# Cross-attention of the samples: values summed on VectorE in PSUM, two heads at a time

## The chip, the cores and the metric

The kernel runs on one core of a Trainium2 chip. The metric is the device time of one execution in microseconds; lower is better. All times below are microseconds unless marked otherwise. TensorE is also called PE, VectorE DVE, ScalarE ACT, GpSimd POOL; SP is the queue that issues most DMAs.

## The reference

One step of a two-layer decoder trunk, f32 throughout, for two groups that share all weights: a prompt of 256 rows and 8 samples of one row each. Each layer is four residual blocks: SwiGLU, a mixer (a gated short convolution in layer 0, a gated linear recurrence in layer 1), cross-attention to a memory of 256 rows, SwiGLU again. What matters here is the cross-attention of the samples, whose keys and values come from a cache, each sample with its own:

```python
def cross_attn(x, mk, mv, w_q, w_o):          # samples: B=8, T=1; mk, mv: (8, 256, 4, 256)
    B, T, D = x.shape
    q = (x @ w_q).reshape(B, T, X_HEADS, X_HEAD_DIM)            # 4 heads of 256
    s = jnp.einsum('bthd,bnhd->bhtn', q, mk) / math.sqrt(X_HEAD_DIM)
    p = jax.nn.softmax(s, axis=-1)
    o = jnp.einsum('bhtn,bnhd->bthd', p, mv).reshape(B, T, D)
    return o @ w_o
```

The prompt does the same against keys and values that are projected from `mem_prompt` in the kernel; those are outputs too.

## The kernel before, in words

Activations stand transposed, `xT[:, k]` holding 128 of the 1024 features over 264 columns: 256 prompt rows, then the 8 samples. Every f32 matrix is split into a high and a low part (`wh`, `wl` of a weight; `xh`, `xl` of an activation), and a product is three matmuls (`mm3`, L326 to L330). Weights arrive in halves of four 128-row blocks: SP loads a half into `raw` (L96), ScalarE rounds it to `wh` (L107), and VectorE or POOL makes `wl` (L120). Which of the two does that is `W.lo`: `("v",)` or `("p",)`.

The order of issue is set by `Flow`. Three lanes hold generators; `flow.tick()` first advances the weights by one split, one round and the loads that fit, and then takes one step of the first generator of each lane. The projections call `tick` once every few matmuls, so other work is spread between them.

The `Ring` has four slots of 1 MB in SBUF (128 x 2048 f32). Its line is fixed: for each layer eight slots of cached keys, eight of cached values, then four of recurrent states. When a slot is given back (`ring.done`) the next load of the line is issued on SP at once. All loads of SP, of weights and of the ring, stand in one queue.

One `attention(l, ...)` runs so:

- `project(XH, ...)` makes the four heads' queries (`qT`). At each head's end `sample_scores(h)` goes to lane 0, and after the last head `sample_rest()`.
- `do_kv(h)`, four times, projects the prompt's keys and values (L930 to L932, tile `kv`) with `W.lo = ("p",)`. Each head ticks eight times, and at its end puts three generators on lane 1: `transpose_k` (tiles `pkt`, `KTt`), `prompt_scores` (`psc`, `mxp`, `Pp`, `ppt`, `PTh`, `PTl`) and `prompt_values` (`po`, then the prompt columns of `oh` and `ol`).
- `sample_scores(h)`: a partition holds 16 of the 256 cached rows of one sample (16 partitions a sample, 8 samples). For each of its 16 rows `i`, VectorE multiplies the key by the query and adds up along the row (L984), giving `sc[:, h, i]`.
- `sample_rest()`: the softmax over `sc` (maxima and sums across a sample's 16 partitions go through small matmuls, tile `pst`). Then `Ps` (L1072) is each weight, divided by the sum and laid out with 8 columns, zero but for the partition's own sample (`own`). TensorE multiplies `Ps[:, h, i]` with the values of row `i` and head `h`, 64 f32 products a layer in four groups (L1086, tile `spv`; a f32 product shows as two records), all into one PSUM bank, head `h` on partitions from 32`h`. ScalarE copies the sums to `os` (L1097), TensorE transposes that (L1101, tile `spt`), and the result goes to the sample columns of `oh` and `ol` (L1104, L1105).
- After the last head `flow.drain(0)` issues what is left of lane 0, `W.lo` goes back to `("v",)`, and `out_proj` (through `project_late`, with `k0` = 6) multiplies `oh` and `ol` by the output weights: the first two chunks over k = 0 to 5, the third over the same, then, once lane 1 is drained (`ready`), k = 6 and 7 of them and the fourth chunk. Columns k = 2h and 2h + 1 belong to head h.

PSUM has eight banks here: four for projections (`mm_bank`) and four for everything else (`aux_bank`); two of the latter hold the third chunk in `project_late`. The framework's scheduler makes the final order on each engine from the order of issue and what is ready, and sets all waits.

Of the kernel before, what the change touches and what calls it, by code (L numbers as in the profile page):

```python
# [8 lines left out]
F32 = mybir.dt.float32  # L9
# [3 lines left out]
ALU = mybir.AluOpType  # L13
# [3 lines left out]
P = 128  # L17
D = 1024
KT = D // P
T = 256  # L20
NB = 8
# [4 lines left out]
XH = 4  # L26
XD = 256
RH = 8
NI = NMEM * NB // P
# [6 lines left out]
HK = 4  # L36
# [203 lines left out]
def trunk_step(ctx: ExitStack, tc: tile.TileContext, ins, consts, outs, stop=None):  # L240
    nc = tc.nc
# [7 lines left out]
    def mm_bank(name):  # L249
        return pmm.tile([P, 512], F32, tag="mm", name=name)  # L250

    def aux_bank(name):
        return paux.tile([P, 512], F32, tag="aux", name=name)

    W = Weights(nc, wp)
    flow = Flow(W)
    ring = Ring(cp)

    ident = cp.tile([P, P], F32, name="ident")
# [4 lines left out]
    own = cp.tile([P, NB], F32, name="own")  # L264
# [67 lines left out]
    class Norm:  # L332
# [55 lines left out]
        def ready(self):  # L388
            if not self.done:
                flow.drain(2)  # L390
# [57 lines left out]
                    evac(c, j, ps[:, :NC])  # L448
                flow.tick()

    def project_late(nch, rh, rl, evac, k0, ready):

        lead = 3
        first = W.chunks[W.pos]
        ws = [W.get_late() for _ in range(lead)]
        pss = [[(mm_bank if c < 2 else aux_bank)(f"pj{c}_{j}") for j in range(2)] for c in range(lead)]

        def block(c, k):
            for j in range(2):
                mm3(pss[c][j][:, :NC], ws[c](k), rh[:, k], rl[:, k], k == 0, k == KT - 1, slice(j * P, j * P + P))  # L460

        for k in range(k0):
            for c in range(2):
                block(c, k)
            if k == HK - 1:
                W.first_live = first[0] + 2
            flow.tick()
        for k in range(k0):
            block(2, k)
            if k == HK - 1:  # L470
                W.first_live = first[1]
            if k % 2:
                flow.tick()
        ready()

        def leave(c, j, ps):
            with tc.high_priority(offset=HURRY):
                evac(c, j, ps[:, :NC])

        def finish(c):  # L480
            for k in range(k0, KT):
                block(c, k)
            W.first_live = first[1] + c + 1
            for j in range(2):
                leave(c, j, pss[c][j])
            flow.tick()

        for c in range(lead - 1):
            finish(c)
        w = W.get_late()  # L490
        for j in range(2):
            ps = mm_bank(f"pj{lead}_{j}")
            for k in range(KT):
                mm3(ps[:, :NC], w(k), rh[:, k], rl[:, k], k == 0, k == KT - 1, slice(j * P, j * P + P))
                if k == KT // 2 - 1:
                    flow.tick()
            if j == 1:
                W.release()
            leave(lead, j, ps)
            flow.tick()  # L500
            if j == 0:
                finish(lead - 1)
# [222 lines left out]
    def add_cache(l):  # L725
        def fill_k(h, hf):
            def f(t):
                rows = ins["cache_mem_k"][l].rearrange("b (g i) h d -> (b g) i h d", i=NI)
                nc.sync.dma_start(t.rearrange("p (i d) -> p i d", d=XD), rows[:, 8 * hf : 8 * hf + 8, h])

            return f

        def fill_v(i2):
            def f(t):
                rows = ins["cache_mem_v"][l].rearrange("b (g i) h d -> (b g) i (h d)", i=NI)
                nc.sync.dma_start(t.rearrange("p (i e) -> p i e", i=2), rows[:, 2 * i2 : 2 * i2 + 2])

            return f

        for h in range(XH):  # L740
            for hf in range(2):
                ring.add((l, "k", h, hf), fill_k(h, hf))
        for i2 in range(NI // 2):
            ring.add((l, "v", i2), fill_v(i2))

    def add_states(key):
        def fill(p):
# [63 lines left out]
    def out_proj(rh, rl, nxt, before=None, late=None):  # L811
        def evac(c, j, ps):
            k = 2 * c + j
            add = nc.vector.tensor_add(xT[:, k], xT[:, k], ps)
            if k == KT - 1:
                W.after["v"] = add.ins
                nxt.low(k - 1)
            nxt.kt(k, low=k != KT - 2)

        if late is not None:  # L820
            project_late(4, rh, rl, evac, *late)
        else:
            project(4, rh, rl, evac, before=before)
# [64 lines left out]
    def attention(l, norm, nxt):  # L888
        with tc.tile_pool(name="at", bufs=1) as ap:
# [3 lines left out]
            oh = ap.tile([P, KT, NC], F32R, name="oh")  # L893
            ol = ap.tile([P, KT, NC], F32R, name="ol")
            sc = ap.tile([P, XH, NI], F32, name="sc")
            Ps = ap.tile([P, XH, NI, NB], F32, name="Ps")
            os = ap.tile([P, XD], F32, name="os")
            nc.gpsimd.memset(os, 0.0)
            tops = ap.tile([P, P], F32, name="tops")
            nc.gpsimd.memset(tops, 0.0)  # L900

# [149 lines left out]
            def sample_rest():  # L1051

                mx, zs, rz = (ap.tile([P, XH], F32, name=n) for n in ("mxs", "zss", "rzs"))
                top = ap.tile([XH, NB], F32, name="top")
                nc.vector.reduce_max(mx, sc, axis=AX.X)
                yield
                pt = aux_bank("pst")
                nc.tensor.transpose(pt[:XH, :P], mx, ident)
                nc.vector.reduce_max(top, pt[:XH, :P].rearrange("h (b g) -> h b g", b=NB), axis=AX.X)
                nc.vector.tensor_copy(tops[:XH].rearrange("h (b g) -> h b g", b=NB), spread(top))  # L1060
                yield
                nc.tensor.matmul(pt[:, P : P + XH], tops, ident[:, :XH], start=True, stop=True)
                nc.vector.tensor_scalar(mx, pt[:, P : P + XH], -1.0 / 16.0, None, op0=ALU.mult)
                for h in range(XH):
                    act(
                        sc[:, h], sc[:, h], AF.Exp, bias=mx[:, h : h + 1], scale=1.0 / 16.0, accum_out=zs[:, h : h + 1]
                    )
                yield
                nc.tensor.matmul(pt[:, P + XH : P + 2 * XH], peers, zs, start=True, stop=True)
                nc.vector.reciprocal(rz, pt[:, P + XH : P + 2 * XH])  # L1070
                for h in range(XH):
                    nc.vector.scalar_tensor_tensor(  # L1072
                        Ps[:, h],
                        sc[:, h].unsqueeze(2).broadcast_to([P, NI, NB]),
                        rz[:, h : h + 1],
                        own.unsqueeze(1).broadcast_to([P, NI, NB]),
                        op0=ALU.mult,
                        op1=ALU.mult,
                    )
                yield  # L1080
                ps = aux_bank("spv")
                for i in range(0, NI, 4):
                    for at in (2, 0, 1, 3):
                        t = ring.tiles[l, "v", (i + at) // 2].rearrange("p (i h d) -> p i h d", i=2, h=XH)
                        for h in range(XH):
                            nc.tensor.matmul(  # L1086
                                ps[32 * h : 32 * h + NB, :XD],
                                Ps[:, h, i + at],
                                t[:, at % 2, h],
                                start=i == 0 and at == 2,  # L1090
                                stop=i == NI - 4 and at == 3,
                            )
                    for i2 in (i // 2, i // 2 + 1):
                        ring.done((l, "v", i2))
                    yield
                for h in range(XH):
                    nc.scalar.copy(os[32 * h : 32 * h + NB], ps[32 * h : 32 * h + NB, :XD])  # L1097
                yield
                pt = aux_bank("spt")
                for dt in range(2):  # L1100
                    nc.tensor.transpose(pt[:, dt * P : dt * P + P], os[:, dt * P : dt * P + P], ident)  # L1101
                ptv = pt[:, : 2 * P].rearrange("p (t h r) -> p h t r", t=2, r=32)[:, :, :, :NB]
                ohv, olv = (t[:, :, T:].rearrange("p (h t) b -> p h t b", t=2) for t in (oh, ol))
                nc.scalar.copy(ohv, ptv)  # L1104
                nc.vector.tensor_sub(olv, ptv, ohv.bitcast(F32))  # L1105

            flow.spawn(1, mem_split())
            project(XH, xh, xl, evac_q, need=norm)
            W.lo = ("p",)
            for h in range(XH):  # L1110
                do_kv(h)
            flow.drain(0)
            W.lo = ("v",)
            out_proj(oh, ol, nxt, late=(KT - 2, lambda: flow.drain(1)))


    GH = 4
# [425 lines left out]
    for i, e in enumerate(plan):  # L1543
        if i + 1 < len(plan):
            nxt = Norm(*plan[i + 1][:3])
        else:
            nxt = Final() if stop is None else Stop()
# [60 lines left out]
```

## Time and profile before

| | us |
|---|---|
| median of 3 runs | 1299.87 (1298.6 to 1300.09) |
| the profiled execution, its own time | 1299.62 |
| its span in the profile | 1297.8 |

The profile is one execution. A group's row gives line, engine, operation, output and inputs with their shapes, the count, then busy us and mean ns of one, then the idle time of the engine just before them and what ended it. A row of an engine's work in order of time gives start, duration, engine, line, operation, output and inputs, count and, in brackets, the idle time before it. Rows of the chain that ended last give start, duration and work. Matmuls overlap, so their pace is read from start to start, not from their durations. The granted TensorE clock was 0.996 over the span.

In layer 0 the attention's kv heads run from 328.2 to 392.8 and out_proj from there to 422.6; in layer 1 the groups `spv` run from 1026.3 to 1050.1.

### The profile page before, as it was taken

To read this page: it belongs to the slowest core of one execution; us is meant where nothing else is said; L and a number is where in the kernel's file an instruction comes from. 1 tells how busy PE (TensorE), PEld (TensorE's weight loads), DVE (VectorE), ACT (ScalarE), POOL (GpSimd) and SP (SyncE) were. 2 spreads that over 40 slices of the span, in tenths; PEclk is the share of its full clock that TensorE was granted. 3 is DMA by queue.
4 is the path that set the end of the run, shared out by engine and by line. 5 is a ranking of instruction groups with operands and counts; after the bars stand their busy time and mean duration, and the time that the engine had idled before them with its cause. 6 is when DMAs were issued, how large, how long until landed. Compare 5 with 4: busy or idle time off the path is not lost.

```text
span 1297.8 us, 25932 instructions
## 1 busy us (share of the span) xinstructions
PE 1276.5 (98%) x10306; PEld 1238.1 (95%) x10306; DVE 824.1 (64%) x1564; ACT 694.3 (53%) x1138; POOL 294.8 (23%) x238
## 2 busy tenths in 40 slices
PE   8999999999999999999999999999999999999997
PEld 8999999999869999999999999999998789999996
DVE  6655567759926755556655545888789637666454
ACT  6455545446545645534554544656675447666542
POOL 3211231212650211132111132000023521211220
PEclk9999999999999999999999999999999999999999
DMA  8695555646998666556566556564557995777650
GB/s 284 225 300 179 168 182 181 196 147 195 360 369 252 187 179 180 179 164 201 178 189 179 173 177 187 163 199 127 179 163 256 399 333 144 232 211 203 202 165 34
DMA packets 263099, 266.75 MB, mean 206 GB/s; under 512 B 8697, under 2 KB 259577, under 8 KB 260930
## 3 DMA queue, kind: packets, MB, share of 16 engines
q1 hardware_dynamic: 257150, 259.78, 64.0%
q10 hardware_dynamic: 5828, 5.32, 1.2%
q8 instruction: 81, 1.33, 0.4%
q14 instruction: 40, 0.33, 0.1%
HBM read 255.00 MB, written 10.07 MB: 204 GB/s over the span
## 4 chain that ended last, share of the span: by engine, by line
PE 92%; DVE 4%; ACT 2%; issue 1%; DMA 0%; POOL 0%; DVEq 0%; SPq 0%; ACTq 0%; POOLq 0%
PE pj L328 19%; PE pj L329 19%; PE pj L330 19%; PE dn L328 7%; PE dn L330 7%; PE dn L329 7%; PE kv L931 2%; PE kv L930 2%; PE kv L932 2%; DVE xl L353 2%; DVE wl L120 1%; PE spv L1086 1%; PE psc L1012 1%; PE pl L1250 1%; PE pj L406 1%
## 5 line engine op out<-in xcount | busy, mean ns | idle before, releaser
L120 DVE TENSOR_TENSOR wl<-raw,wh 128x1024 fp32r<-128x1024 f32 (+1 forms) x347 | 426.3, 1233 | 245.9 <-ACT wh L107 231.4
L328 PE MATMUL pj<-xh,wh 128*128 128x264 f32 x1952 | 558.7, 286 | 5.1 <-DVE qT L916 2.5
L329 PE MATMUL pj<-xl,wh 128*128 128x264 f32 x1952 | 553.2, 284 | 0.0
L330 PE MATMUL pj<-xh,wl 128*128 128x264 f32 x1952 | 552.9, 283 | 0.0
L107 ACT CAST wh<-raw 128x1024 fp32r<-128x1024 f32 (+1 forms) x406 | 416.3, 1032 | 253.1 <-PE pj L329 128.4
L328 PEld LDWEIGHTS pj<-xh,wh 128*128 128x128 f32 x1952 | 367.7, 188 | 7.3 <-DVE qT L916 3.0
L329 PEld LDWEIGHTS pj<-xl,wh 128*128 128x128 f32 x1952 | 367.9, 189 | 0.0
L330 PEld LDWEIGHTS pj<-xh,wl 128*128 128x128 f32 x1952 | 366.1, 188 | 0.0
L328 PE MATMUL dn<-ah,wh 128*128 128x264 f32 x704 | 200.9, 285 | 0.0
L330 PE MATMUL dn<-ah,wl 128*128 128x264 f32 x704 | 200.0, 284 | 0.0
L329 PE MATMUL dn<-al,wh 128*128 128x264 f32 x704 | 199.4, 283 | 0.0
L780 POOL TENSOR_TENSOR al<-a,ah 128x264 fp32r<-128x264 f32 x88 | 90.2, 1026 | 418.8 <-ACT ah L779 418.7
L120 POOL TENSOR_TENSOR wl<-raw,wh 128x1024 fp32r<-128x1024 f32 (+1 forms) x61 | 142.8, 2350 | 183.9 <-ACT wh L107 122.3
L330 PEld LDWEIGHTS dn<-ah,wl 128*128 128x128 f32 x704 | 132.7, 188 | 0.0
L328 PEld LDWEIGHTS dn<-ah,wh 128*128 128x128 f32 x704 | 132.4, 188 | 0.2
L329 PEld LDWEIGHTS dn<-al,wh 128*128 128x128 f32 x704 | 132.5, 188 | 0.0
L308 ACT ACTIVATE g<-g 128x264 f32<-128x264 f32 x88 | 37.0, 424 | 80.7 <-DVE g L772 80.5
L779 ACT CAST ah<-a 128x264 fp32r<-128x264 f32 x88 | 36.0, 413 | 65.2 <-DVE a L778 65.0
L348 ACT ACTIVATE xh<-xT,gains 128x264 fp32r<-128x264 f32 x56 | 28.2, 513 | 74.2 <-DVE xT L806 59.2
L984 DVE CUSTOM_DVE_ANT_0 junk<-ring,pq 128x256 f32<-128x256 f32 x128 | 53.7, 419 | 3.7
L778 DVE TENSOR_TENSOR a<-g,pj 128x264 f32<-128x264 f32 x88 | 37.1, 426 | 28.7 <-PE pj L330 28.6
L772 DVE TENSOR_TENSOR g<-pj,R_norm_ffn 128x264 f32<-128x264 f32 x88 | 37.5, 429 | 25.7 <-PE pj L330 25.3
(330 smaller groups left out, 1495.6 us busy)
## 6 DMA issues: line engine op xcount, KB each, us to landing
raw<-in_w_ffn_gate_dram SPq DMA_DIRECT2D x88, 512.0 KB, 4.7
raw<-in_w_ffn_up_dram SPq DMA_DIRECT2D x88, 512.0 KB, 4.0
raw<-in_w_ffn_down_dram SPq DMA_DIRECT2D x64, 512.0 KB, 3.5
ring<-in_cache_mem_k_dram SPq DMA_DIRECT2D x16, 1024.0 KB, 8.2
raw<-in_w_xkv_dram SPq DMA_DIRECT2D x64, 256.0 KB, 3.7
ring<-in_cache_mem_v_dram SPq DMA_DIRECT2D x16, 1024.0 KB
raw<-in_w_rec_in_dram SPq DMA_DIRECT2D x32, 512.0 KB, 4.6
raw<-in_w_ffn_down_dram SPq DMA_DIRECT2D x32, 384.0 KB, 3.0
```

Of the source, the lines that this page charges most:

```text
L107: self.pin(self.behind(self.hi[i % len(self.hi)], copy(wh[:, :n], self.raw[i][:, :n])))
L120: ins = eng.tensor_sub(wl[:, :n], self.raw.pop(i)[:, :n], wh[:, :n].bitcast(F32))
L308: in_line(nc.scalar.activation(dst, src, func, **kw))
L328: nc.tensor.matmul(ps, wh[:, s], rh, start=first, stop=False)
L329: nc.tensor.matmul(ps, wh[:, s], rl, start=False, stop=False)
L330: nc.tensor.matmul(ps, wl[:, s], rh, start=False, stop=last)
L348: W.pin(nc.scalar.activation(xh[:, k, :n], src, AF.Copy, scale=gcol(self.name, self.layer, k)))
L772: nc.vector.tensor_mul(g, ps, norm.R)
L778: nc.vector.tensor_mul(a, g, ps)
L779: nc.scalar.copy(ah[:, blk], a)
L780: nc.gpsimd.tensor_sub(al[:, blk], a, ah[:, blk].bitcast(F32))
L984: nc.vector.tensor_tensor_reduce(junk, t[:, i % 8], pq[:, :XD], 1.0, 0.0, ALU.mult, ALU.add, sc[:, h, i : i + 1])
```

## The change

TensorE no longer multiplies `Ps` with the values. For each pair of heads VectorE keeps two running sums side by side in one PSUM bank (`acc`): row by row `i`, and head by head within it, it multiplies the values with the partition's own weight `sc[:, h, i]` and adds the sum so far. The last row's result goes to SBUF (`total`). That leaves one sum for each partition, 16 for a sample; four f32 products a pair, with `total` as the weights and the 8 columns of `oz` (one over the softmax's sum in the partition's own sample, zero elsewhere), add those up across partitions and transpose at once. The copies to `oh` and `ol` follow for each pair.

A slot of cached values now holds four rows of two heads and not two rows of four heads, so that a pair needs four slots. `flow.drain(0)` is gone: `project_late` asks for pair 0 before k = 0 and for pair 1 before k = 4, through `until`, and does k = 0 to 3 of all three chunks before k = 4 and 5. `W.lo` changes to `("v",)` only at the second of these.

```diff
-    def project_late(nch, rh, rl, evac, k0, ready):
+    def project_late(nch, rh, rl, evac, k0, need, ready):
...
-        for k in range(k0):
-            for c in range(2):
-                block(c, k)
-            if k == HK - 1:
-                W.first_live = first[0] + 2
-            flow.tick()
-        for k in range(k0):
-            block(2, k)
-            if k == HK - 1:
-                W.first_live = first[1]
-            if k % 2:
+        for a, b in ((0, HK), (HK, k0)):
+            need(a)
+            for k in range(a, b):
+                for c in range(2):
+                    block(c, k)
+                if k == HK - 1:
+                    W.first_live = first[0] + 2
                 flow.tick()
+            for k in range(a, b):
+                block(2, k)
+                if k == HK - 1:
+                    W.first_live = first[1]
+                if k % 2:
+                    flow.tick()
         ready()
...
-        def fill_v(i2):
+        def fill_v(pair, i4):
             def f(t):
                 rows = ins["cache_mem_v"][l].rearrange("b (g i) h d -> (b g) i (h d)", i=NI)
-                nc.sync.dma_start(t.rearrange("p (i e) -> p i e", i=2), rows[:, 2 * i2 : 2 * i2 + 2])
+                at = slice(2 * pair * XD, 2 * pair * XD + 2 * XD)
+                nc.sync.dma_start(t.rearrange("p (i e) -> p i e", i=4), rows[:, 4 * i4 : 4 * i4 + 4, at])
...
-                for h in range(XH):
-                    nc.vector.scalar_tensor_tensor(Ps[:, h], ...)
+                nc.vector.tensor_mul(
+                    oz,
+                    rz.unsqueeze(2).broadcast_to([P, XH, NB]),
+                    own.unsqueeze(1).broadcast_to([P, XH, NB]),
+                )
                 yield
-                ps = aux_bank("spv")
-                for i in range(0, NI, 4):
...
-                            nc.tensor.matmul(
-                                ps[32 * h : 32 * h + NB, :XD],
-                                Ps[:, h, i + at],
-                                t[:, at % 2, h],
...
+                for pair in range(XH // 2):
+                    acc = aux_bank("acc")
+                    total = ap.tile([P, 2, XD], F32, tag="total", name="total", bufs=1)
+                    for i in range(NI):
+                        t = ring.tiles[l, "v", pair, i // 4].rearrange("p (i h d) -> p i h d", i=4, h=2)
+                        for j in range(2):
+                            p, sums = sc[:, 2 * pair + j, i : i + 1], acc[:, j * XD : j * XD + XD]
+                            if i == 0:
+                                nc.vector.tensor_scalar(sums, t[:, i % 4, j], p, None, op0=ALU.mult)
+                            else:
+                                dst = total[:, j] if i == NI - 1 else sums
+                                nc.vector.scalar_tensor_tensor(
+                                    dst, t[:, i % 4, j], p, sums, op0=ALU.mult, op1=ALU.add
+                                )
+                        if i % 4 == 3:
+                            ring.done((l, "v", pair, i // 4))
+                        if i % 2:
+                            yield
+                    pt = aux_bank("spt")
+                    for j in range(2):
+                        for dt in range(2):
+                            at = (2 * j + dt) * NB
+                            nc.tensor.matmul(
+                                pt[:, at : at + NB],
+                                total[:, j, dt * P : dt * P + P],
+                                oz[:, 2 * pair + j],
+                                start=True,
+                                stop=True,
+                            )
+                    ptv = pt[:, : 4 * NB].rearrange("p (t b) -> p t b", b=NB)
+                    ohv, olv = (t[:, 4 * pair : 4 * pair + 4, T:] for t in (oh, ol))
+                    nc.scalar.copy(ohv, ptv)
+                    nc.vector.tensor_sub(olv, ptv, ohv.bitcast(F32))
+                    sampled.add(pair)
                     yield
+
+            def until(pair):
+                while pair not in sampled:
+                    flow.step()
+                if pair:
+                    W.lo = ("v",)
...
-            flow.drain(0)
-            W.lo = ("v",)
-            out_proj(oh, ol, nxt, late=(KT - 2, lambda: flow.drain(1)))
+            out_proj(oh, ol, nxt, late=(KT - 2, lambda k: until(k // 4), lambda: flow.drain(1)))
```

More of the change, by code (lines that the diff above doesn't have):

```diff
@@ L742, in add_cache @@
                 ring.add((l, "k", h, hf), fill_k(h, hf))
-        for i2 in range(NI // 2):
-            ring.add((l, "v", i2), fill_v(i2))
+        for pair in range(XH // 2):
+            for i4 in range(NI // 4):
+                ring.add((l, "v", pair, i4), fill_v(pair, i4))
     def add_states(key):
@@ L895, in attention @@
             sc = ap.tile([P, XH, NI], F32, name="sc")
-            Ps = ap.tile([P, XH, NI, NB], F32, name="Ps")
-            os = ap.tile([P, XD], F32, name="os")
-            nc.gpsimd.memset(os, 0.0)
+            oz = ap.tile([P, XH, NB], F32, name="oz")
+            sampled = set()
             tops = ap.tile([P, P], F32, name="tops")
@@ L1070, in sample_rest @@
                 nc.vector.reciprocal(rz, pt[:, P + XH : P + 2 * XH])
-                for h in range(XH):
[L1072 to L1079, printed above, removed]
-                yield
@@ L1081, in sample_rest @@
-                ps = aux_bank("spv")
-                for i in range(0, NI, 4):
[L1083 to L1086, printed above, removed]
-                                ps[32 * h : 32 * h + NB, :XD],
-                                Ps[:, h, i + at],
-                                t[:, at % 2, h],
-                                start=i == 0 and at == 2,
-                                stop=i == NI - 4 and at == 3,
-                            )
-                    for i2 in (i // 2, i // 2 + 1):
-                        ring.done((l, "v", i2))
-                    yield
@@ L1096, in sample_rest @@
[L1096 to L1103, printed above, removed]
@@ L1104, in sample_rest @@
-                nc.scalar.copy(ohv, ptv)
-                nc.vector.tensor_sub(olv, ptv, ohv.bitcast(F32))
+                nc.vector.tensor_mul(
[3 more added lines that the diff above has]
+                )
+                yield
+                for pair in range(XH // 2):
+                    acc = aux_bank("acc")
[19 more added lines that the diff above has]
+                            at = (2 * j + dt) * NB
+                            nc.tensor.matmul(
+                                pt[:, at : at + NB],
[3 more added lines that the diff above has]
+                                stop=True,
+                            )
+                    ptv = pt[:, : 4 * NB].rearrange("p (t b) -> p t b", b=NB)
[3 more added lines that the diff above has]
+                    sampled.add(pair)
+                    yield
```

## The prediction, made before the run

> **What bounds the kernel now.** I read the page's busy shares and the chain first, then the stretches of layer 0's attention, then each engine in order of time there. Layer 1's attention holds the same groups of instructions, so every term counts twice.
>
> ```profile
> PE 1276.5 (98%) x10306; PEld 1238.1 (95%) x10306; DVE 824.1 (64%) x1564; ACT 694.3 (53%) x1138; POOL 294.8 (23%) x238
> PE 92%; DVE 4%; ACT 2%; issue 1%; DMA 0%; POOL 0%; DVEq 0%; SPq 0%; ACTq 0%; POOLq 0%
> ```
>
> TensorE holds 92% of the chain: work taken off it shortens the run, unless another engine becomes late. The samples' products are such work:
>
> ```profile
> L1086 PE MATMUL spv<-ring,Ps 128*8 128x256 f32 x256 | 15.3, 379 | 0.0
> ```
>
> Where they run, VectorE is nearly free (columns: busy us of PE, PEld, DVE, ACT, POOL, then clock, DMA share, GB/s):
>
> ```profile
> 360.00:370.00 10.00, 10.00 (x93) 6.34 (x92) 3.99 (x10) 3.20 (x13) 3.90 (x2) 1.00 1.07 408
> 370.00:380.00 10.00, 10.00 (x64) 7.96 (x67) 2.08 (x3) 6.21 (x10) 5.30 (x3) 1.00 1.01 411
> 380.00:390.00 10.00, 9.97 (x88) 6.55 (x77) 0.18 (x1) 3.77 (x7) 6.62 (x3) 1.00 1.03 274
> 390.00:400.00 10.00, 10.00 (x70) 9.17 (x70) 5.01 (x11) 4.93 (x12) 0.00 (x0) 1.00 1.17 321
> 400.00:410.00 10.00, 10.00 (x79) 9.79 (x78) 5.74 (x10) 4.33 (x9) 0.00 (x0) 1.00 1.01 341
> ```
>
> TensorE has no gap from 360 to 410, and VectorE is busy for 11.3 of the 40 us to 400. The DMA engines are full throughout. So the question is whether that free VectorE time, 28.7 us, holds the new sums before TensorE asks for them.
>
> **The change part by part.** Off TensorE: eight groups of products (four a layer), and the two transposes of `os`.
>
> ```profile
> 359.32 0.38 PE L1062 MATMUL pst<-ident,tops 128*128 128x4 f32 x2 [0.16 <-DVE tops L1060]
> 359.56 0.48 PE L931 MATMUL kv<-wl,mh 128*128 128x512 f32 x1
> ...
> 363.00 0.39 PE L931 MATMUL kv<-wl,mh 128*128 128x512 f32 x1
> 363.23 0.40 PE L932 MATMUL kv<-wh,ml 128*128 128x512 f32 x1
> 363.56 1.91 PE L1086 MATMUL spv<-ring,Ps 128*8 128x256 f32 x32
> 365.40 0.50 PE L930 MATMUL kv<-wh,mh 128*128 128x512 f32 x1
> ...
> 388.68 0.39 PE L930 MATMUL kv<-wh,mh 128*128 128x512 f32 x1
> 389.10 0.44 PE L1101 MATMUL spt<-ident,os 128*128 128x128 f32 x2
> 389.37 0.60 PE L960 MATMUL pkt<-ident,Kn 128*128 128x128 f32 x4
> ...
> 392.82 0.28 PE L328 MATMUL pj<-oh,wh 128*128 128x264 f32 x1
> 422.51 0.28 PE L330 MATMUL pj<-oh,wl 128*128 128x264 f32 x1
> ```
>
> From start to start, 363.23 to 365.40 is 2.17; less one product of kv (0.23, 363.00 to 363.23) a group costs 1.94. The transposes: 389.37 - 388.68 - 0.23 = 0.46. A layer loses 4 x 1.94 + 0.46 = 8.2.
>
> On to TensorE: four products a pair with `total` as the weights and 8 columns, each f32 product being two records (as L1062 is). The nearest row is L1062: two records from 359.32 to 359.56, 0.12 each. 8 x 0.12 = 0.96 a pair, 1.9 a layer. The net is 6.3 a layer, 12.6 in all.
>
> On to VectorE: 64 instructions a layer over 128x256, two heads in turn, each reading its own last sum. No VectorE instruction of before writes PSUM; the nearest rows:
>
> ```profile
> L353 DVE SCALAR_TENSOR_TENSOR xl<-px,gains,xh 128x256 fp32r<-128x256 f32 x8 | 3.3, 472 | 0.2 <-ACT xh L348 0.2
> 310.70 1.27 DVE L908 SCALAR_TENSOR_TENSOR ml<-memT,gains,mh 128x256 fp32r<-128x256 f32 x3
> 312.03 0.43 DVE L319 SCALAR_TENSOR_TENSOR nacc_norm_xattn<-ps_ms,R_norm_xattn 128x264 f32<-128x264 f32 x1
> 312.50 0.43 DVE L323 SCALAR_TENSOR_TENSOR nacc_norm_xattn<-nacc_norm_xattn,R_norm_xattn 128x264 f32<-128x264 f32 x1
> 362.26 1.14 DVE L1072 SCALAR_TENSOR_TENSOR Ps<-sc,rzs,own 128x128 f32<-128x128 f32 x4
> ```
>
> One takes 0.472, from PSUM as from SBUF. Three that need nothing of each other take 1.27, so they follow at (1.27 - 0.47) / 2 = 0.40. One that needs its predecessor follows at 0.47 after a duration of 0.43, that is 0.04 behind its end: 0.51 for this shape. These are the two ends. I take 0.40, the lower: with two heads in turn the sum that an instruction needs was begun 0.80 earlier, and the L1072 rows, all into one tile, overlap too (four in 1.14). 64 x 0.40 = 25.6; the four Ps (1.14) go, one small product (`oz`) comes.
>
> [...]
>
> The rest of VectorE's work between 362.3 and the moment the second pair is wanted:
>
> ```profile
> L964 DVE COPY KTt<-pkt 128x512 f32<-128x512 f32 x8 | 5.5, 687 | 1.5 <-PE pkt L960 1.5
> L996 DVE TENSOR_REDUCE mxp<-psc 128x2 f32<-128x512 f32 x8 | 5.5, 690 | 6.3 <-PE psc L1012 6.3
> L997 DVE TENSOR_SCALAR mxp<-mxp 128x2 f32<-128x2 f32 x8 | 2.2, 272 | 0.2
> L1004 DVE TENSOR_SCALAR Pp<-Pp,zsp 128x256 f32<-128x256 f32 x16 | 7.1, 488 | 0.2
> L1033 DVE TENSOR_TENSOR PTl<-ppt,PTh 128x512 fp32r<-128x512 f32 x8 | 5.5, 690 | 12.9 <-ACT PTh L1032 12.9
> L948 DVE TENSOR_TENSOR Vl<-Vn,Vh 128x512 fp32r<-128x512 f32 x8 | 5.5, 689 | 6.9 <-ACT Vh L947 6.9
> L1049 DVE TENSOR_TENSOR ol<-po,oh 128x512 fp32r<-128x512 f32 x8 | 5.5, 682 | 1.5 <-ACT oh L1048 1.5
> ```
>
> Head 1 from mxp to ol: 0.69 + 0.27 + 0.98 + 0.69 + 0.68 = 3.3. Head 2 the same with KTt: 4.0. Vl of heads 2 and 3: 1.4. Head 3's KTt and mxp: 1.65. `oz`, reciprocals and the small `ol`, an estimate of 1.0 from L997's size. Together 11.3. The sums then end at 362.3 + 25.6 + 11.3 = 399.2, and with the last pair's products (0.96) and the copies to oh and ol (0.5, an estimate from the smallest rows above) the second pair is there at about 400.7.
>
> TensorE asks for it at k = 4 of out_proj:
>
> ```profile
> 397.29 0.44 PE pkt L960 x4
> 400.01 1.73 PE psc L1012 x8
> ...
> 409.35 0.28 PE L328 MATMUL po<-PTh,Vh 128*128 128x256 f32 x1
> 410.77 0.29 PE L328 MATMUL pj<-oh,wh 128*128 128x264 f32 x1
> ```
>
> out_proj began at 392.82; less 8.2, plus the first pair's 0.96, it begins at 385.6. Three chunks over k = 0 to 3 are 72 products at 0.12 each (po's twelve, below, take 1.42), 8.7. Work that also lies in front: head 2's transposes (0.44, as pkt) and po (1.42), head 3's pkt and psc (0.44 + 1.73), 4.0. So 398.3, and a stall of 2.4 us. The first pair (half the sums, head 1 and Vl: about 381) is in time for 385.6.
>
> A layer gains 6.3 - 2.4 = 3.9, net 7.8. The profiled execution took 1299.62 (span 1297.8 and 1.8 around it), 0.25 under the median: 1291.8, against a median of about 1292.
>
> The smaller edits. Order of issue, counted in `flow.step`: 9 steps until the first kv head, 32 in the kv heads; the scores take 24, `sample_rest` 4, each pair 9. Pair 0 ends at step 37 of 41 and pair 1 at step 46, one of the six ticks between the two `need` calls; so `need` forces no bunching. Halves split between them move to POOL:
>
> ```profile
> L120 DVE TENSOR_TENSOR wl<-raw,wh 128x1024 fp32r<-128x1024 f32 (+1 forms) x347 | 426.3, 1233 | 245.9 <-ACT wh L107 231.4
> L120 POOL TENSOR_TENSOR wl<-raw,wh 128x1024 fp32r<-128x1024 f32 (+1 forms) x61 | 142.8, 2350 | 183.9 <-ACT wh L107 122.3
> ```
>
> Some two a layer: 1.1 later each, on a POOL at 0.00 from 390 to 410, and 2.5 off VectorE where it helps nothing counted above. The four copies of `os`, the memset and Ps leave ACT and POOL, which nobody waits for.
>
> SP's queue: a slot is freed by VectorE's last read, not by TensorE.
>
> ```profile
> 365.10 5.17 SPq L736 DMA_DIRECT2D ring<-in_cache_mem_v_dram  x4
> 380.74 11.27 SPq L751 DMA_DIRECT2D ring<-in_state_rec_dram  x8
> ```
>
> Pair 1's four loads now leave one by one, about every 4.6 us ((25.6 + 11.3) / 8) from 367; the state loads, until now from 380.74 to 392, wait until about 385 to 399, and the first FFN weights queue behind the last. They are wanted when out_proj ends, at about 417 (422.5 less 3.9 and a split's 1.2), so some 15 us cover them; without that cover the delay would be the seven us by which the state loads move.
>
> **The rivals.** (A) The forecast: 1291.8.
>
> (B) The sums run one behind the other, because both heads lie in one PSUM tile and each waits for the one before: 0.51 in place of 0.40, 7.0 us a layer more, less about 1 where other VectorE work fills the gaps. The stall is 8.4, a layer loses 2.1, and the run takes 1303.8: slower. It decides from (6.3 - 2.4) / 64 = 0.06 more per instruction, at 0.46. For it: L323 waits for L319. Against it: L1072 overlaps within a tile. [...]
>
> (C) VectorE starves on pair 1's values. The loads for TensorE's third group left from 365.10 and it ran 14 us later, with DMA full:
>
> ```profile
> 379.27 1.84 PE spv L1086 x32
> ```
>
> Pair 1 wants its first slot, which leaves at about 367, at about 381, after half of the sums and the work between them. The slots now move in 2 KB pieces, not 8 KB. That leaves nothing to spare; I take two us late a layer: 1295.8.
>
> (D) The stall is hidden, as other TensorE work (head 3's transposes, later blocks) fills it: 1299.62 - 12.6 = 1287.0.
>
> **How the numbers follow.** A 0.40, B 0.35, C 0.15, D 0.10. 0.2% is 2.6 us, about what a measurement of this kernel tells from no change. A and D are faster almost whole (0.49), C by 0.09 of its 0.15; B is slower by 0.25 and within by 0.10. Faster 0.58, same 0.17, slower 0.25. The range is from just under D to B: 1286.5 to 1304.5; A's own is 1287 to 1297.
>
> **What would show it.** The acc instructions' spacing (0.40 or 0.51); no spv and two short spt groups a layer; DVE at 9 to 10 of 10 us from 362 to 400; a wait of TensorE at out_proj's k = 4 for ol or oh of 2 to 3 us; state loads issued until about 399. Wrong would make me: spacing over 0.46, waits of VectorE for the v loads, or TensorE queued behind a transpose that waits for VectorE inside the kv heads.

## The result, and the profile after

The changed kernel is slower: 1311.54 us (median of four runs, 1310.06 to 1312.58) against 1299.95 for the kernel before on the same chip, a ratio of 1.0094 with a 95% interval of 1.0082 to 1.0107. The forecast was 1291.8, its range ended at 1304.5. The profiled execution took 1310.64, span 1308.9, granted clock 0.989 (before: 0.996).

The page's busy shares, and the group of the sums:

```profile
PE 1269.1 (97%) x10078; PEld 1240.9 (95%) x10078; DVE 878.9 (67%) x1682; ACT 691.5 (53%) x1132; POOL 308.8 (24%) x242
L1091 DVE SCALAR_TENSOR_TENSOR acc<-ring,sc,acc 128x256 f32<-128x256 f32 x112 | 54.4, 486 | 2.5
```

TensorE lost 228 records and still the run grew. Layer 0's attention by stretches (columns as before):

```profile
360.00:370.00 10.00, 9.52 (x50) 7.83 (x49) 9.37 (x22) 5.26 (x13) 5.21 (x3) 1.00 1.07 396
380.00:390.00 10.00, 9.07 (x59) 7.73 (x58) 9.59 (x19) 5.32 (x12) 4.30 (x3) 1.00 0.83 285
390.00:400.00 10.00, 9.01 (x68) 8.58 (x66) 9.05 (x21) 4.36 (x8) 5.97 (x3) 1.00 1.03 287
400.00:410.00 10.00, 2.85 (x14) 2.88 (x15) 7.34 (x13) 0.22 (x3) 1.26 (x1) 0.68 0.84 238
410.00:420.00 10.00, 10.00 (x69) 9.96 (x69) 2.17 (x4) 2.14 (x4) 0.00 (x0) 0.81 0.71 210
```

VectorE is as full as forecast (9 to 9.6 from 380 to 400), but it is not done at 399: from 400 to 410 TensorE has 2.85 us of work, and the clock, 1.00 everywhere before, falls to 0.68 and is still at 0.81 in the next stretch, where TensorE is busy throughout. The list of waits (us in total, times, longest), and TensorE in order of time around the gap:

```profile
PE spt L1102 <- DVE total L1091: 17.6, 4, 8.1
398.72 0.28 PE L330 MATMUL pj<-oh,wl 128*128 128x264 f32 x1
407.15 1.84 PE L1102 MATMUL spt<-oz,total 128*128 128x8 f32 x8 [8.14 <-DVE total L1091]
410.18 0.42 PE L330 MATMUL pj<-oh,wl 128*128 128x264 f32 x1
410.40 0.42 PE L328 MATMUL pj<-oh,wh 128*128 128x264 f32 x1
413.70 0.32 PE L328 MATMUL pj<-oh,wh 128*128 128x264 f32 x1
413.86 0.29 PE L329 MATMUL pj<-ol,wh 128*128 128x264 f32 x1
413.98 0.28 PE L330 MATMUL pj<-oh,wl 128*128 128x264 f32 x1
```

After the gap products of the same shape stand 0.22 apart (410.18 to 410.40), and only from 413.7 again 0.12. The clock granted in narrower stretches says the same; it fell while TensorE was still waiting:

```profile
403.50:407.15 3.65, 0.00 (x0) 0.03 (x1) 3.44 (x8) 0.00 (x0) 0.00 (x0) 0.50 0.63 176
407.15:413.70 6.55, 6.55 (x30) 6.55 (x31) 1.13 (x3) 0.77 (x2) 0.00 (x0) 0.50 1.17 316
```

So 6.55 us, from 407.15 to 413.70, ran at half pace, some 3.3 us lost on top of the wait. Layer 1 has the same wait of 8.14.

VectorE and GpSimd in order of time:

```profile
362.64 2.06 DVE L1091 SCALAR_TENSOR_TENSOR acc<-ring,sc,acc 128x256 f32<-128x256 f32 x4
368.57 3.10 DVE L1091 SCALAR_TENSOR_TENSOR acc<-ring,sc,acc 128x256 f32<-128x256 f32 x6
...
380.86 1.22 DVE L1007 TENSOR_SCALAR Pp<-Pp,zsp 128x256 f32<-128x256 f32 x1
382.00 0.86 DVE L1091 SCALAR_TENSOR_TENSOR total<-ring,sc,acc 128x256 f32<-128x256 f32 x2
382.78 1.98 DVE L1007 TENSOR_SCALAR Pp<-Pp,zsp 128x256 f32<-128x256 f32 x1
...
398.71 0.35 DVE L1007 TENSOR_SCALAR Pp<-Pp,zsp 128x256 f32<-128x256 f32 x1
399.36 2.05 DVE L1007 TENSOR_SCALAR Pp<-Pp,zsp 128x256 f32<-128x256 f32 x1
401.73 1.21 DVE L120 TENSOR_TENSOR wl<-raw,wh 128x1024 fp32r<-128x1024 f32 x1
402.86 3.63 DVE L1091 SCALAR_TENSOR_TENSOR acc<-ring,sc,acc 128x256 f32<-128x256 f32 x7
406.52 0.87 DVE L1091 SCALAR_TENSOR_TENSOR total<-ring,sc,acc 128x256 f32<-128x256 f32 x2
```

```profile
379.53 2.40 POOL L120 TENSOR_TENSOR wl<-raw,wh 128x1024 fp32r<-128x1024 f32 x1 [2.11 <-ACT wh L107]
382.25 2.37 POOL L120 TENSOR_TENSOR wl<-raw,wh 128x1024 fp32r<-128x1024 f32 x1 [0.32 <-ACT wh L107]
396.42 4.84 POOL L120 TENSOR_TENSOR wl<-raw,wh 128x1024 fp32r<-128x1024 f32 x2 [4.03 <-ACT wh L107]
```

Two things are to be read here. One sum lasts 0.49, so six in 3.10 stand (3.10 - 0.49) / 5 = 0.522 apart and seven in 3.63 stand 0.523: each begins when the one before has ended, the rival's spacing. This holds where one sum stands right behind another, which 37 of the 64 a layer do; 35 of these begin 0.51 to 0.53 after the one before. Where other VectorE work follows a sum, it begins 0.39 after the sum's start (a sum at 398.97, the Pp at 399.36). And a Pp takes 0.35 alone, but three take 1.22, 1.98 and 2.05, each ending within 0.2 of the end of a wl on GpSimd (381.93, 384.62, 401.26). The second pair's sums end at 407.39 and not at 399.2.

### The profile page after: what moved, and what is told of

Its sections match the earlier page's. It is cut to its first block, busy times and chain, and to the rows that moved or that the text cites. A ratio compares the mean times of both kernels' runs of the same rounds, so it can differ in the third digit from the quotient of the medians.

```text
span 1308.9 us, 25606 instructions
## 1 busy us (share of the span) xinstructions
PE 1269.1 (97%) x10078; PEld 1240.9 (95%) x10078; DVE 878.9 (67%) x1682; ACT 691.5 (53%) x1132; POOL 308.8 (24%) x242
## 4 chain that ended last, share of the span: by engine, by line
PE 90%; DVE 5%; ACT 2%; issue 1%; POOL 0%; DMA 0%; DVEq 0%; SPq 0%; ACTq 0%; POOLq 0%
PE pj L328 19%; PE pj L329 19%; PE pj L330 19%; PE dn L328 7%; PE dn L330 7%; PE dn L329 6%; PE kv L934 2%; PE kv L935 2%; PE kv L933 2%; DVE acc L1091 1%; PE psc L1015 1%; DVE xl L353 1%; PE pl L1263 1%; PE pj L406 1%; DVE wl L120 1%
## 5 line engine op out<-in xcount | busy, mean ns | idle before, releaser
L120 DVE TENSOR_TENSOR wl<-raw,wh 128x1024 fp32r<-128x1024 f32 (+1 forms) x341 | 418.7, 1232 | 237.9 <-ACT wh L107 224.3
L120 POOL TENSOR_TENSOR wl<-raw,wh 128x1024 fp32r<-128x1024 f32 x67 | 157.3, 2357 | 196.2 <-ACT wh L107 162.1
L1091 DVE SCALAR_TENSOR_TENSOR acc<-ring,sc,acc 128x256 f32<-128x256 f32 x112 | 54.4, 486 | 2.5
```

The costliest lines, as they stand in the source:

```text
L120: ins = eng.tensor_sub(wl[:, :n], self.raw.pop(i)[:, :n], wh[:, :n].bitcast(F32))
L1091: nc.vector.scalar_tensor_tensor(dst, t[:, i % 4, j], p, sums, op0=ALU.mult, op1=ALU.add)
```

## The experiments

Three explanations stand against each other or side by side: the sums wait for each other because two heads share a PSUM bank; VectorE is held up by GpSimd; and the slow clock after the wait. Edits are to the changed kernel unless said.

**Each head's sums in a bank of their own.**

```
-  acc = aux_bank("acc")
+  acc = [aux_bank("acc") for _ in range(2)]
-  ..., acc[:, j * XD : j * XD + XD]
+  ..., acc[j][:, :XD]
```

> One bank for each head's sum instead of one for both. Theory 'shared bank' (the two sums run one behind the other because they lie in one PSUM tile): the instructions follow at 0.40 us instead of 0.525, the second pair ends 8 us earlier a layer (about 399 in layer 0), TensorE's wait before the pair's products shrinks from 8.1 us to under 2 and the clock does not fall; about 1292 us. Rival 'PSUM write' (an instruction that writes PSUM takes 0.52 wherever it writes): spacing and wait stay, within 2 us of 1311.5.

1297.79 us, ratio 0.9991 [0.9981, 1.0001]. VectorE, GpSimd and TensorE in order of time:

```profile
393.10 3.22 DVE L1091 SCALAR_TENSOR_TENSOR acc<-ring,sc,acc 128x256 f32<-128x256 f32 x8
397.22 1.82 DVE L1000 TENSOR_SCALAR mxp<-mxp 128x2 f32<-128x2 f32 x1
399.35 0.86 DVE L1091 SCALAR_TENSOR_TENSOR total<-ring,sc,acc 128x256 f32<-128x256 f32 x2
```

```profile
394.34 4.69 POOL L120 TENSOR_TENSOR wl<-raw,wh 128x1024 fp32r<-128x1024 f32 x2 [2.05 <-ACT wh L107]
```

```profile
399.88 0.39 PE L328 MATMUL pj<-oh,wh 128*128 128x264 f32 x1 [2.71 <-DVE total L1091]
402.22 0.42 PE L328 MATMUL pj<-oh,wh 128*128 128x264 f32 x1
402.44 0.42 PE L329 MATMUL pj<-ol,wh 128*128 128x264 f32 x1
405.19 0.28 PE L329 MATMUL pj<-ol,wh 128*128 128x264 f32 x1
405.31 0.28 PE L330 MATMUL pj<-oh,wl 128*128 128x264 f32 x1
```

Eight sums stand (3.22 - 0.48) / 7 = 0.39 apart: the shared bank made the 0.13. But the time only came back to that of the kernel before, where 1292 was expected. The sums ended at 400.21, 7.2 sooner than in the changed kernel; 4.8 of that is the spacing (the 64 sums take 25.8 us of VectorE in place of 30.5, each counted to the next start), and most of the rest is that head 3's Pp and a wl now come after the last sum. TensorE waited 2.71 a layer, and behind that wait its products stood 0.22 apart from about 401.5 to 405.0 (clock 0.83 from 400 to 410), 0.12 ahead of it: another 1.7. A `mxp` over two elements, 0.16 when alone, took 1.82, up to the end of GpSimd's wl (397.22 + 1.82 = 399.04; 394.34 + 4.69 = 399.03).

**The scalings Pp on ScalarE**, one bank as in the changed kernel.

```
-  nc.vector.tensor_scalar(pr[:, r], pr[:, r], zs[:, r : r + 1], None, op0=ALU.mult)
+  nc.scalar.activation(pr[:, r], pr[:, r], AF.Copy, scale=zs[:, r : r + 1])
```

> The prompt's softmax scaling (Pp, 16 instructions) moves from VectorE to ScalarE; the shared bank stays. Theory 'POOL in the way' (Pp takes up to 2.05 us where POOL works at the same time, in front of the sums): about 7 us of VectorE time a layer go after 362, the second pair ends at about 401, the wait falls to about 2 us; about 1294 us. Rival 'spacing alone': the sums still follow at 0.525, and the wait shrinks by the plain cost of six Pp, 2 us; about 1305 us.

1304.83 us, ratio 1.0047 [1.0029, 1.0065], the time of the rival. The sums stay 0.52 apart and end at 404.2, 3.2 sooner, not the 6 or so of the theory; the wait is 5.9:

```profile
PE spt L1102 <- DVE total L1091: 11.7, 2, 5.9
399.17 2.18 DVE L120 TENSOR_TENSOR wl<-raw,wh 128x1024 fp32r<-128x1024 f32 x1
395.55 4.72 POOL L120 TENSOR_TENSOR wl<-raw,wh 128x1024 fp32r<-128x1024 f32 x2 [3.52 <-ACT wh L107]
```

Now a wl of VectorE's own, 1.21 when alone, takes 2.18: it ends at 401.35, 1.08 after the end of GpSimd's (400.27), as if it had first waited for that. So part of the hold-up only moved.

**Half the rows** (rows 8 to 15 of the cached values are left out of the sums; all loads stay).

```
-  for i in range(NI):
+  for i in range(NI // 2):
```

> Leaves out rows 8 to 15 of each partition's values (32 of the 64 instructions a layer); the loads and everything else stay. If VectorE's lateness and what follows from it are the whole loss, TensorE has no wait and the whole of its saving shows: 1287 us. If the other edits (order of the blocks, 2 KB pieces, later state loads) cost something by themselves, the time stays above that by it.

1288.54 us, ratio 0.9927 [0.9912, 0.9943]. With VectorE in time TensorE does not wait for the sums at all (only for Pp, 3.7 in all) and 10.2 us are gained; the clock is 1.00 from 400 to 420. The other edits (slots, `until`, wl on GpSimd) therefore cost little in themselves: 10.2 is 2.4 short of what was forecast for TensorE.

**Only one pair on VectorE** (heads 0 and 1; heads 2 and 3 through Ps and TensorE as before, their 32 products after the first pair's).

```
-  for pair in range(XH // 2):
+  for pair in range(1):
...
+      nc.tensor.matmul(ps[q : q + NB, :XD], Ps[:, j, 4 * i4 + i], t[:, i, j], ...)
```

> Heads 0 and 1 on VectorE as in the changed kernel, heads 2 and 3 on TensorE as before, in the new slots. TensorE saves half (4 us a layer, less about 1 for the products that add up), VectorE carries 32 instructions a layer and has them done at about 382. Theory 'VectorE late for the second pair': no wait, about 1294 us. Rival 'the first pair is late too' (it stopped the kv heads for about 1 us at 382): about 1297 us.

1312.01 us, ratio 1.0102 [1.0086, 1.0118]: a miss. The list of waits shows where:

```profile
PE ppt L1035 <- DVE Pp L1013: 5.1, 5, 2.0
PE spt L1117 <- DVE total L1106: 4.9, 2, 2.4
```

The first pair's sums, still 0.52 apart, were now themselves waited for inside the kv heads (2.4 a layer), transposes waited for held-up Pp, and the clock was 0.89 and 0.77 from 380 to 400. How much each of these took was not separated.

**Both heads' sums in one tile in SBUF.**

```
-  acc = aux_bank("acc")
+  acc = ap.tile([P, 2 * XD], F32, tag="accs", name="accs", bufs=1)
```

> The running sums of both heads lie in one tile in SBUF instead of one bank of PSUM, all else as in the changed kernel. If it is the shared PSUM bank that makes each sum wait for the one before (0.523 us apart), sums in one SBUF tile stand about 0.40 apart wherever GpSimd is idle. If it is the shared tile (a wait that goes by the tile, not by the memory), they stand 0.52 apart here too. In both cases an instruction now reads two operands from SBUF: if GpSimd's wl work holds up such instructions, single sums last 1 to 2.4 us while a wl runs on GpSimd (10 us of it from 380 to 400), and the sums end no sooner than 403: 1303 to 1320 us; if GpSimd holds up only the Pp form, they end near 400 and the time is 1298 us as with two banks.

1319.09 us, ratio 1.0155 [1.0135, 1.0175]. The group by form (ns min/median/max), then VectorE and GpSimd in order of time:

```profile
L1091 DVE SCALAR_TENSOR_TENSOR accs<-ring,sc,accs x112: 448/477/2631, 362.1 to 1083.0; 128x256 f32<-128x256 f32 x112
390.62 7.11 DVE L1091 SCALAR_TENSOR_TENSOR accs<-ring,sc,accs 128x256 f32<-128x256 f32 x7
398.26 2.85 DVE L1091 SCALAR_TENSOR_TENSOR accs<-ring,sc,accs 128x256 f32<-128x256 f32 x7
390.75 5.12 POOL L120 TENSOR_TENSOR wl<-raw,wh 128x1024 fp32r<-128x1024 f32 x2 [5.02 <-ACT wh L107]
```

With GpSimd idle seven sums take 2.85, (2.85 - 0.48) / 6 = 0.395 apart, in one tile: so a shared tile alone does not make them wait; in PSUM it was the bank. With two wl on GpSimd beside them seven take 7.11, and a single sum takes up to 2.63, where two of GpSimd's wl, at 380.43 and 383.10, took 2.40 and 2.63. So sums with two operands in SBUF were held up; those of the changed kernel, with one operand in PSUM, never took over 0.491. Most of the time lost is waits of TensorE inside the kv heads, 9.5 us for Pp and 7.6 for PTl, with 3.9 for the sums.

**The wait filled.**

```
+  for _ in range(60 * pair):
+      nc.tensor.matmul(pt[:, P : P + NC], oh[:, 0, :P], oh[:, 0], start=True, stop=True)
```

> The changed kernel, with 60 matmuls of no use (128x128 by 264 columns, into unused columns of the second pair's product bank, nothing reads them) issued on TensorE just ahead of the second pair's products, so about 7 us of the 8.1 us in which TensorE waits for the sums are filled, 60 x 0.12. Theory (the clock fell because TensorE stood idle, and the slow matmuls after it cost about 3 us a layer): matmuls after the wait go at 0.12 apart from the first, the clock is 1.00 in 410 to 420, and the time is about 1305 us, 6 less than the changed kernel, though 120 matmuls are added. Rival (the clock falls for another reason than idleness, or the slow stretch is made up later): 1311 us or more. If the fill were longer than the wait, up to 1 us a layer is added.

1304.82 us, ratio 1.0045 [1.003, 1.006]: 120 useless products made the changed kernel faster, by 6.7 us between the medians and by 5.4 with each taken against its own runs of the kernel before.

```profile
398.32 7.54 PE L1100 MATMUL spt<-oh 128*128 128x264 f32 x60
406.16 1.06 PE L1104 MATMUL spt<-oz,total 128*128 128x8 f32 x8 [0.30 <-DVE total L1091]
407.28 0.28 PE L329 MATMUL pj<-ol,wh 128*128 128x264 f32 x1
407.40 0.28 PE L330 MATMUL pj<-oh,wl 128*128 128x264 f32 x1
400.00:410.00 10.00, 9.70 (x81) 9.49 (x80) 7.32 (x13) 1.72 (x3) 1.37 (x1) 1.00 0.91 248
```

The clock stays at 1.00 and the products after the wait stand 0.12 apart at once. The sums ended 0.9 sooner a layer than in the changed kernel (406.50 in layer 0), as the wl at 401.73 came after them, so the clock's own part lies between some 3.6 us (5.4 less 1.8) and the 6.6 read from the slow stretches (3.3 a layer).

**All wl of the attention on VectorE.**

```
-  W.lo = ("p",)
+  W.lo = ("v",)
```

> The changed kernel, with the subtractions wl that GpSimd does during the cross-attention (from its four heads to the second pair's sums) put on VectorE, so that GpSimd does nothing beside the sums. Theory (an instruction of VectorE of the Pp form is held up while GpSimd runs a wl): every Pp takes 0.34 us, none over 0.5, which gives back about 5 us of the three long ones (1.98, 2.05, 1.22 us), and VectorE takes on 6 wl of 1.2 us up to 399, 7.2 us: sums end at 409 to 411, 1313 to 1320 us. Rival (Pp is long for another reason, such as its operands on ScalarE's side or the DMAs): Pp still up to 2 us, sums end at 414 or later, 1323 us or more.

1348.78 us, ratio 1.0384 [1.0363, 1.0404].

```profile
L1007 DVE TENSOR_SCALAR Pp<-Pp,zsp x16: 346/348/351, 349.4 to 1107.0; 128x256 f32<-128x256 f32 x16
PE spt L1102 <- DVE total L1091: 36.4, 4, 9.8
```

With GpSimd idle (busy 0.00 from 360 to 430) every Pp takes 0.35: the hold-up was GpSimd's. The time was missed by far: the halves of the kv heads before 362 also went to VectorE, the sums began at 376.6 in place of 359.3, and TensorE waited 36.4.

**Two banks and Pp on ScalarE**, both edits together.

> Each head's sums in a bank of their own, and the two scalings of the prompt's probabilities (Pp) on ScalarE. Theory (all that the change lost is VectorE's lateness, made of 0.12 us more on each sum instruction and of VectorE work held up by GpSimd): with separate banks the sums ended at 400.2 and TensorE waited 2.7 us; with Pp on ScalarE alone they ended 3.2 us sooner than in the changed kernel; both together end near 397, TensorE does not wait, its clock stays at 1.00 in 400 to 410, and the time is 1288 to 1291 us, near the 1288.5 of the kernel that leaves out half the rows. Rival (GpSimd holds up whatever VectorE then has in flight, so taking Pp away only moves the hold-up to wl and others): sums end at 399 to 400, a wait of 1 to 2.5 us a layer remains, 1294 to 1297 us.

1286.84 us, ratio 0.9906 [0.989, 0.9923]: faster than both kernels, at the forecast's PE term.

```profile
400.00:410.00 10.00, 10.00 (x85) 9.96 (x84) 4.79 (x7) 4.32 (x9) 0.68 (x1) 1.00 1.11 314
395.99 0.87 DVE L1091 SCALAR_TENSOR_TENSOR total<-ring,sc,acc 128x256 f32<-128x256 f32 x2
```

The sums end at 396.86, before TensorE asks; it has no gap from 400 to 410 and its clock stays at 1.00. Against their own runs of the kernel before, the changed kernel is at +11.6 us, separate banks alone at -0.9, Pp on ScalarE alone at +6.1, both at -11.8: 23.4 together, 12.5 and 5.5 alone. That is more than their sum; either edit alone leaves a wait and the slow stretch behind it.

**The kernel before with Pp on ScalarE**, a control.

> The kernel before, with only the two scalings of the prompt's probabilities (Pp) put on ScalarE, a control for the 1286.8 us of the kernel with two banks and this edit. Theory (VectorE does not set the end in the kernel before, so relieving it alone brings nothing; the gain comes from the sums on VectorE once they are in time): 1297.5 to 1300 us, ratio 0.999 to 1.001. Rival (the edit itself gains, by taking away the Pp instructions of up to 1.5 us ahead of the transposes ppt): 1293 to 1296 us.

1301.79 us, ratio 1.0021 [1.0011, 1.0031]: no gain there, but a loss of 2.8 us, more than was expected (a Pp takes 0.51 on ScalarE, 0.35 on VectorE when alone; where the 2.8 arise was not followed). So the 11.8 us of the kernel with two banks come from the sums on VectorE, once they are in time.

**One head after the other within a slot**, otherwise the kernel of 1286.84.

```
-  for i in range(NI):
-      for j in range(2):
+  for i4 in range(0, NI, 4):
+      for j in range(2):
+          for i in range(i4, i4 + 4):
```

> Two banks and Pp on ScalarE as in the kernel of 1286.8 us, but the rows of a slot are added for one head and then for the other, so that three of four sums read what the instruction just before wrote. Theory (a sum starts when the one before it has ended if both work in one bank): groups of four stand at 2.06 us as in the changed kernel, 0.52 apart, though there are two banks; the sums end about 5 us later than with heads in turn, near 402, TensorE waits 3 to 5 us a layer and its clock falls for some us after it; 1298 to 1304 us. Rival (it is the number of open banks or tiles that sets the spacing, not what the instruction before touched): groups of four take 1.66 us, 1287 us.

1290.08 us, ratio 0.9934 [0.9914, 0.9954].

```profile
368.74 3.22 DVE L1092 SCALAR_TENSOR_TENSOR acc<-ring,sc,acc 128x256 f32<-128x256 f32 x8
PE pj L329 <- DVE ol L1112: 1.6, 2, 0.8
```

Still 0.39 apart, but this decides nothing on the spacing: in the list of instructions as built the two heads' sums stand in turn again but for a few, since the framework's scheduler had put the independent sums between the dependent ones. What the edit changed is only when the work is offered; 0.8 a layer of wait for the last `ol` is part of the some 3 us lost.

## Why the prediction was wrong

*TensorE's term was right.* Forecast: 12.6 less. From after: 17.6 of wait for the sums and 3.6 to 6.6 of slow clock, less 11.6 of loss in all, leave 9.6 to 12.6 saved. The kernel that does not wait saves 11.8, the one with half the rows 10.2.

*When TensorE asks was right.* Forecast 398.3; its last product ahead of the wait began at 398.72.

*The step that failed: 362.3 + 25.6 + 11.3 = 399.2, the end of the sums, and in it first "64 x 0.40".* The rows gave 0.40 and 0.51 as ends, and the lower was taken because the sum that an instruction needs had begun 0.80 earlier. Measured 0.523 behind another sum in one bank, 0.39 in two. That is rival B's mechanism: two heads in one PSUM bank made each sum wait for the one before though it does not need it. In the instructions as built most sums of the changed kernel (70 of the 112 `acc`) wait for the VectorE instruction just before; with two banks none does, most wait for the one before that. But it is not paid 64 times: 35 sums a layer begin late, by 0.13 each, 4.6 us. The 64 took 30.5 us where 25.6 were forecast, 4.9 more; B had 7.0, less 1 for gaps. That B's wait of 8.4 met the 8.14 measured is therefore in part luck, for the rest came from elsewhere (below). The argument against B, from the L1072 rows, did not bear: those lie in one SBUF tile, as in the experiment with sums in SBUF (0.395), not in one bank. Whether a bank would hold up the second sum without that wait was not tried, since the framework sets the waits. In two banks a sum of 0.48 begins 0.39 after the one before.

*The other term, 11.3 for the rest of VectorE's work, failed by more.* The sums began 3.0 sooner than reckoned (359.31) and ended 8.2 later (407.39): 48.1 us where 36.9 were forecast. The sums are 4.9 of the 11.2. Pp is 4.7: four were counted at their mean of before, 2.0 together, and head 3's two not at all, but all six fell before the end and took 6.6, of which 5.0 were hold-ups by GpSimd (0.8 for the pair at 365.13, then 0.9, 1.6 and 1.7). A wl on VectorE at 401.73 is 1.1, and VectorE stood idle 2.1, mostly for `mxp`'s and `zsp`'s inputs; both were put at nothing. The rest of the work came out 1.6 smaller.

*A term was missing: the clock after a wait.* B was priced at 8.4 a layer and the wait measured 8.14, yet B's 1303.8 fell 7.7 short. The slow stretch after the wait accounts for 3.6 to 6.6 of that, and the first pair's wait of 0.68 a layer for 1.4. It also spoils the forecast's own case: with two banks A's spacing came true and its stall of 2.4 was 2.7, but the time was 1297.8, for 1.7 a layer went to the clock and TensorE waited 2.2 in all for Pp. The runs show the size of the term: after a wait of 8.14 TensorE ran 6.55 us at half pace (granted clock 0.50 from 407.15 to 413.70), and with two banks, after a wait of 2.71, some 3.5 us (products 0.22 apart in place of 0.12).

*A cost put at nothing was not: VectorE beside GpSimd.* The prediction let two halves of wl a layer go to a GpSimd that was "at 0.00 from 390 to 410" and put no cost on it in the sum. GpSimd made three more in layer 0 (20 in place of 17), ran 5.97 us of 390 to 400 and held up a Pp by 1.7 us there. Two more Pp were held up by 0.9 and 1.6 at 380.86 and 382.78, beside halves ahead of these; the kernel before has Pp of up to 1.47 too, in its row's mean of 488 against 0.35 alone, but there no engine waited for Pp. The runs show what was held up: a Pp of the changed kernel took up to 2.05 in place of 0.35 and ended within 0.2 of the end of GpSimd's wl, a mxp with two banks 1.82 in place of 0.16 and ended with it to 0.01, VectorE's own wl with Pp on ScalarE 2.18 in place of 1.21 and ended 1.08 after it, and sums with two operands in SBUF took up to 2.63 in place of 0.48; the sums in PSUM never took over 0.491.

*Rival C did not come.* VectorE idled for the sums' inputs only 0.9 us in all, and for ScalarE's `sc`, never for the loads. *D* has the number of the kernel with both edits, 1287.0 and 1286.84, but not its mechanism: no other TensorE work fills a wait there, the sums are in time. Against its own runs of the kernel before, that kernel gains 11.8 where D had 12.6. *The first pair* was forecast for 381 and called in time for 385.6; its sums ended at 382.86, and TensorE, which has the pair's products among those of the kv heads, waited 0.68. Transposes inside the kv heads waited for Pp as well, 1.5 us in all: the last sign named for being wrong, though small. *State loads* left until 407.42 rather than 399, and no wait for them shows.

## What to carry to other kernels

When sums move to VectorE, keep those that run in turn in different PSUM banks: with two in one bank each waited for the one before here (0.52 apart against 0.39). Price a wait of the bounding engine at more than its length: here 8.1 us of wait cost some 10 to 11, and 2.7 some 4.4, so a forecast that ends with "a stall of 2.4" has to add the slow clock behind it. And before work is moved to an idle GpSimd, list the VectorE instructions that lie beside it: here a Pp (`tensor_scalar`) took up to 2.05 in place of 0.35, a wl 2.18 in place of 1.21 and sums with two operands in SBUF up to 2.63 in place of 0.48, and no sum with one operand in PSUM took over 0.491.

## What was not expected of the hardware

After a TensorE wait of 2.71 us its pace was halved for some 3.5 us (products 0.22 apart in place of 0.12), after one of 0.68 it was not (clock 1.00 from 382 to 387); 60 products a layer that nobody reads, in place of the wait, made the run some 6 us faster. A `tensor_scalar` over two elements a partition took 1.82 us in place of 0.16 beside a GpSimd subtraction, and ended with it to 0.01 us.
